# A hybrid decoder block: attention with the orders of three engines written out, and the gates' first products ahead for seven pairs

## The chip, the cores and the metric

The kernel runs on one core of one Trainium2 chip. Its time is device microseconds of one execution; lower is better. A core has a matmul engine (PE, TensorE; its weight loads are listed as PEld), VectorE (DVE), ScalarE (ACT), GpSimd (POOL), SyncE (SP), which only issues DMAs here, and 16 DMA engines. Matmuls read operands from SBUF and write banks of 128 x 512 float32 in PSUM.

## The reference

One layer, 1024 positions, width 1024, all float32:

```python
h = _rmsnorm(x, g_mix_pre[l])
proj = jnp.einsum('bsd,de->bse', h, w_in[l]) + b_in[l]
u_pool, q, k, v, gates = jnp.split(proj, IN_SPLITS, axis=-1)
y_pool = _multiscale_pool(u_pool, w_pool[l], pool_scale[l])
...
y_attn = _sliding_window_sink_attention(
    q.reshape(B, S, N_KV_HEADS, GROUP, HEAD_DIM), k, v, attn_sinks[l])
g = jax.nn.sigmoid(gates.astype(jnp.float32)).astype(x.dtype)
g_pool, g_attn = g[..., :D_MODEL], g[..., D_MODEL:]
merged = (g_pool * jnp.einsum('bsc,cd->bsd', y_pool, w_branch_pool[l])
          + g_attn * jnp.einsum('bsc,cd->bsd', y_attn, w_branch_attn[l]))
mix = jnp.einsum('bsd,de->bse', merged, w_out[l])
x = x + _rmsnorm(mix, g_mix_post[l])
h2 = _rmsnorm(x, g_mlp_pre[l])
ff = jnp.einsum('bsf,fd->bsd',
                jnp.square(jax.nn.relu(jnp.einsum('bsd,df->bsf', h2, w_up[l]))), w_down[l])
x = x + _rmsnorm(ff, g_mlp_post[l])
```

Attention has 8 query heads and 2 key heads of 64, a window of 128 in blocks of 128, and a sink per head in the softmax. The pooling takes, for each of four groups of 128 channels, the mean over the last 2, 4, 8 or 16 positions less the input, and mixes it with a 128 x 128 matrix.

## The kernel before

**Precision.** Every float32 matrix product is done in three passes (hi x hi, hi x lo, lo x hi) of a shorter type, `PASSES`. `split(hi, lo, src)` makes the parts: ScalarE casts (L101), VectorE subtracts (L104), so each operand costs one instruction on either engine, and VectorE's waits for ScalarE's.

**Stages.** The first stage multiplies x by the weights of q, k and v (L179, L188), tiles 0 to 3 while the weights come in. The attention stage (from about 44 us in the profile) takes eight tiles n of 128 positions. `pre_qkv(n)` scales and rotates on VectorE and GpSimd; `post_qkv(n)` transposes q and k and splits them; `score(n, g)` makes scores for one half (g = 0, 1) of the heads, four in number, in a PSUM bank called "sc", of which there is one. ScalarE copies the part of the tile's own keys out of it (L325), and VectorE's copy_predicated (L326) lays the previous tile's keys over it where the mask says so; only then is the bank free for the next half. `softmax(n)` takes maxima on VectorE, eight exponentials on ScalarE (L340), and scales on VectorE (L343). `attend_t(n)` transposes the probabilities (L354), splits them, and multiplies them with a mask (L360); `attend_v(n)` multiplies by v (L369), and ScalarE copies the result to y (L373).

Between these steps `fill(t)` takes matmuls worth t us from a generator, `others()`: q, k and v of tiles 4 to 7, then the products u for the pooling (L538; groups gi = 3, 2, 1, 0, of windows 16, 8, 4, 2), each with a VectorE multiplication (L541) and a ScalarE bias (L542).

`pool_in(gi)` forms the windowed sums of one u on VectorE by doubling (L606, L607), subtracts (L609 to L611) and splits the result; `pool_mix(gi)` multiplies with the mixing matrix (L622 to L624), scales on ScalarE (L625) and spills to DRAM.

**Gates.** The gates' projection (2048 outputs) is done by an algorithm of seven block products for each pair p = 0 to 7 of weight blocks (`class Pairs`). Products 1 and 2 take x itself, the others sums and differences of x that `build_gate(kt)` makes in four steps from freshly loaded x (L678 to L684). `prepare(p)` loads a weight block and splits the operands of products 1 and 2. `m1(p)` is product 1 (12 matmuls, L461); ScalarE copies its bank to f0 (L468, the changed kernel's L487). `m2(p)` adds product 2 on top in the same bank, and VectorE scales the sum into f0. `rest(p)` does the other five products (60 matmuls). For pairs 0 to 4 (`NG0 = 5`) m1 and m2 stand ahead, among pooling and `build_gate`: this stretch, from about 182 to 225 us, is called the gate front here. Pairs 5 to 7 do all seven in the loop of rests, which begins at 225 us. After the gates come the branches, the output product and the MLP, which are the same in both kernels.

**Order.** In the attention stage a `manual_schedule` holds PE to the order in which the code stands; VectorE, ScalarE and the whole gate front are ordered by the framework's scheduler. Each engine then works through its queue in order. The results f0 take slots of a pool "yy" of four, which y and the pooling sums also use. DMAs are issued by SyncE's queue, or by ScalarE's (`nc.scalar.dma_start`).

Of the kernel before, what the change touches and what calls it, by code (L numbers as in the profile page):

```python
# [14 lines left out]
P = 128  # L15
# [35 lines left out]
def block_kernel(ctx: ExitStack, tc, xt, x, consts, vecs, sinks, b_qkv, g_post, g_mlp, g_mlp_post,  # L51
# [227 lines left out]
    def post_qkv(n):  # L279
        tf = tfs.pop(n)  # L280
        t = tf[:, :768].rearrange("p (h d) -> p h d", d=HD)
        bt, bk = bank("at"), bank("at")
# [24 lines left out]
    def score(n, g):  # L307
# [18 lines left out]
        dve.copy_predicated(s4, wide(from_prev), sb[:, :, :, :P] if n else wide(neg))  # L326

    soft = {}

    def softmax(n):  # L330
# [7 lines left out]
        act.activation(es, es, AF.Exp)  # L338
        for h in range(NH):
            act.activation(s8[:, h], s8[:, h], AF.Exp, scale=SCALE, bias=nmx[:, h:h + 1], accum_out=den[:, h:h + 1])  # L340
        dve.tensor_tensor(den, den, es, ALU.add)
# [5 lines left out]
    def attend_t(n):  # L347
# [8 lines left out]
        pc = None  # L356
        if n:
            pc = [at("s4", 4, [NH, P], F32R) for _ in range(2)]
            for t, s in zip(pc, pt):
                dve.tensor_tensor(t, f32(s), own_t.unsqueeze(1).broadcast_to([P, NH, P]), ALU.mult)  # L360
        probs[n] = pt, pc
# [146 lines left out]
    us, wu = {}, {}  # L508
# [3 lines left out]

    def others():
        for qs, kvs in (((4,), (4,)), ((5,), (5,)), ((6, 7), (6, 7))):
            for n in qs:
                bq[n] = bank("mm")
                for k in range(NK):
                    mm_q(n, k, bq[n])
                    yield 3 * 0.227
            if n == NT - 1:  # L520
                wu[3] = load_w(w_u[3], [NK, P])
            for n in kvs:
                bkv[n] = bank("at" if n == 4 else "mm", [1, 256])
                for k in range(NK):
                    mm_kv(n, k)
                    yield 3 * 0.12
                pre_qkv(n)
        for gi in (3, 2, 1, 0):
            if gi:
                wu[gi - 1] = load_w(w_u[gi - 1], [NK, P])  # L530
            whi, wlo = wu.pop(gi)
            u = ga_.tile([P, S], F32, tag="ga", name=nm("u"))
            for th in range(2):
                sl = slice(th * 512, (th + 1) * 512)
                b = bank("mm")
                for k in range(NK):
                    for j, (xh, h) in enumerate(PASSES):
                        pe.matmul(b, (whi, wlo)[h][:, k, :], xr(k, xh, th), start=k == 0 and j == 0,  # L538
                                  stop=k == NK - 1 and j == 2)
                    yield 3 * 0.227  # L540
                dve.tensor_tensor(u[:, sl], b, rb[:, sl], ALU.mult)  # L541
            act.activation(u, u, AF.Identity, bias=vec[:, V_BU + gi:V_BU + gi + 1])  # L542
            us[gi] = u
# [13 lines left out]
    with tc.manual_schedule(engines={mybir.EngineType.PE}):  # L557
        for n in range(4):
            pre_qkv(n)
        fill(8.3)  # L560
        post_qkv(0)
        make_rb()
        score(0, 0)
        fill(2.5)
        post_qkv(1)
        score(0, 1)
        softmax(0)
        fill(3.0)
        score(1, 0)
        fill(2.5)  # L570
        post_qkv(2)
        score(1, 1)
        softmax(1)
        fill(5.5)
        for n in range(NT):
            attend_t(n)
            fill(2.5)
            if n + 2 < NT:
                score(n + 2, 0)
            fill(2.0)  # L580
            if n + 2 < NT:
                score(n + 2, 1)
                softmax(n + 2)
            if n + 3 < NT:
                post_qkv(n + 3)
            fill(2.5)
            attend_v(n)
            if n % 4 == 3:
                for kh in range(2):
                    nc.sync.dma_start(y_dram[n // 4 * 2 + kh], flat(y[n // 4][kh]))  # L590
        fill(1e3)


    wps = stage([4, P])
    nc.sync.dma_start(wps, w_pool)
# [114 lines left out]
    for p in (3, 4):  # L710
        gt.m1(p, bank("mm"), g32([S]))
        gt.m2(p)
# [563 lines left out]
```

## Time and profile before

| | |
|---|---|
| median of 3 runs | 1154.15 us (1153.27 to 1158.45) |
| profiled execution | 1154.03 us, of which the span of instructions is 1152.2 us |
| PE | 1120.7 us busy (97%), 5202 matmuls |
| VectorE, ScalarE | 820.4 us (71%), 525.1 us (46%) |
| GpSimd | 70.0 us (6%) |
| DMA | 179.06 MB, mean 155 GB/s |

A row of a timeline gives start and duration in us, engine, line, operation and tiles, the count, and in brackets the idle time before it with the instruction that ended it. A row of waits gives engine, tile and line that waited, what it waited for, us in total, times, and the longest. In a row of a group of instructions, the total busy time and the mean ns of one follow the bar. Durations overlap a little where instructions of one engine are pipelined; what counts is the distance from one start to the next. PEclk is the clock granted to TensorE, 1.00 at full speed. Lines are those of the kernel before unless said otherwise.

### The profile page before, as it was taken

What the parts mean: (1) busy time and instruction counts of PE and PEld (TensorE: products, weight loads), DVE (VectorE), ACT (ScalarE), POOL (GpSimd) and SP (SyncE); (2) the same over time, 40 slices, a digit from 0 to 9 for tenths busy, and PEclk for the clock granted to TensorE, in tenths of its full rate; (3) what the DMA queues carried; (4) which work ended last, traced back from release to release, by engine and by line L of the source; (5) the groups of instructions that cost most, each with busy time, mean ns of one, the idle gap of its engine ahead of it and who ended that gap; (6) DMA issues with size and microseconds to landing.
All of it is one profiled execution on the core that took longest, in us unless ns stands there. A gap on an engine that the chain in (4) does not pass through costs nothing.

```text
span 1152.2 us, 13954 instructions
## 1 busy us (share of the span) xinstructions
PE 1120.7 (97%) x5202; PEld 925.8 (80%) x5202; DVE 820.4 (71%) x1209; ACT 525.1 (46%) x912; POOL 70.0 (6%) x110
## 2 busy tenths in 40 slices
PE   7999998899999999999999999999999999999997
PEld 6877776788888888888788888888888888888885
DVE  7677797998654585767997766666557945446887
ACT  7354556544332233364655444535344345344342
POOL 3523110000000150000000000000000000000000
PEclk9999999999999999999999999999999999999999
DMA  7210106544345453333256434343788665432652
GB/s 261 74 46 19 56 19 249 189 165 146 123 168 185 149 199 110 139 127 120 92 220 219 170 132 177 125 179 123 266 296 290 222 194 180 130 92 73 205 190 99
DMA packets 66163, 179.06 MB, mean 155 GB/s; under 512 B 6192, under 2 KB 6192, under 8 KB 66096
## 3 DMA queue, kind: packets, MB, share of 16 engines
q1 hardware_dynamic: 60336, 157.73, 39.8%
q10 hardware_dynamic: 5760, 20.45, 4.5%
q8 instruction: 41, 0.67, 0.2%
q14 instruction: 26, 0.21, 0.1%
HBM read 127.82 MB, written 50.33 MB: 155 GB/s over the span
## 4 chain that ended last, share of the span: by engine, by line
PE 85%; DVE 9%; ACT 3%; DMA 2%; issue 1%; SPq 0%; DVEq 0%
PE mm L461 20%; PE at L461 16%; PE at L1114 14%; PE mm L1114 11%; PE mm L831 5%; PE mm L398 5%; PE mm L179 3%; PE mm L400 3%; PE at L188 1%; PE sc L179 1%; DVE s L360 1%; ACT s L340 1%; PE at L831 1%; PE mm L538 1%; PE sc L323 1%
## 5 line engine op out<-in xcount | busy, mean ns | idle before, releaser
L1114 PE MATMUL at<-ar,wh 128*128 128x512 f32 x744 | 169.5, 389 | 0.0
L1114 PEld LDWEIGHTS at<-ar,wh 128*128 128x128 f32 x744 | 139.6, 188 | 29.3 <-DVE ar L104 0.4
L1114 PE MATMUL mm<-ar,wh 128*128 128x512 f32 x576 | 131.0, 389 | 0.0
L1114 PEld LDWEIGHTS mm<-ar,wh 128*128 128x128 f32 x576 | 108.1, 188 | 22.5
L101 ACT CAST wh<-st 128x512 fp32r<-128x512 f32 (+1 forms) x106 | 67.0, 642 | 123.7 <-PE mm L398 34.1
L104 DVE TENSOR_TENSOR wh<-raw,wh 128x1024 fp32r<-128x1024 f32 x53 | 64.8, 1223 | 80.9 <-ACT wh L101 80.5
L101 ACT CAST wh<-raw 128x1024 fp32r<-128x1024 f32 x53 | 55.8, 1053 | 131.1 <-PE at L1114 62.6
L104 DVE TENSOR_TENSOR wh<-st,wh 128x512 fp32r<-128x512 f32 (+1 forms) x106 | 82.9, 788 | 16.4 <-ACT wh L101 14.0
L461 PE MATMUL mm<-gr,wh 128*128 128x512 f32 x300 | 72.1, 390 | 0.0
L461 PE MATMUL mm<-T,wx 128*128 128x512 f32 x288 | 67.6, 389 | 0.0
L461 PEld LDWEIGHTS mm<-gr,wh 128*128 128x128 f32 x300 | 56.1, 188 | 11.6
L461 PEld LDWEIGHTS mm<-T,wx 128*128 128x128 f32 x288 | 54.1, 188 | 11.2
L461 PE MATMUL at<-T,wx 128*128 128x512 f32 x252 | 59.1, 389 | 0.0
L461 PE MATMUL mm<-x,wh 128*128 128x512 f32 x216 | 52.5, 399 | 3.5 <-ACT g L468 3.5
L461 PEld LDWEIGHTS at<-T,wx 128*128 128x128 f32 x252 | 47.3, 188 | 9.8
L461 PEld LDWEIGHTS mm<-x,wh 128*128 128x128 f32 x216 | 41.6, 193 | 12.8 <-ACT g L468 3.9
L104 DVE TENSOR_TENSOR ar<-B,ar 128x1024 fp32r<-128x1024 f32 x37 | 45.0, 1217 | 9.4 <-ACT ar L101 9.4
L538 PE MATMUL mm<-x,wh 128*128 128x512 f32 x192 | 48.7, 404 | 0.0
L461 PE MATMUL at<-gr,wh 128*128 128x512 f32 x183 | 44.2, 389 | 0.0
L101 ACT CAST ar<-B 128x1024 fp32r<-128x1024 f32 x37 | 38.8, 1050 | 11.1 <-DMA B<-in_w_dn_dram 6.2
L538 PEld LDWEIGHTS mm<-x,wh 128*128 128x128 f32 x192 | 35.7, 192 | 7.6
L748 DVE TENSOR_TENSOR g<-g,mm 128x512 f32<-128x512 f32 x32 | 20.5, 683 | 28.3 <-PE mm L400 28.2
(350 smaller groups left out, 2204.3 us busy)
## 6 DMA issues: line engine op xcount, KB each, us to landing
raw<-f_dram SPq DMA_DIRECT2D x53, 512.0 KB, 3.6
f_dram<-g SPq DMA_DIRECT2D x30, 512.0 KB, 3.3
B<-in_w_dn_dram SPq DMA_DIRECT2D x24, 512.0 KB, 5.7
st<-in_w_up_dram SPq DMA_DIRECT2D x22, 512.0 KB, 3.5
f_dram<-g ACTq DMA_DIRECT2D x17, 512.0 KB, 2.6
st<-in_w_g_dram SPq DMA_DIRECT2D x16, 512.0 KB, 3.8
g<-spill_dram SPq DMA_DIRECT2D x16, 512.0 KB, 4.3
raw<-in_w_dn_dram SPq DMA_DIRECT2D x16, 512.0 KB, 4.5
```

The lines of the kernel that those rows point to most:

```text
L101: act.copy(hi, src)
L104: eng.tensor_tensor(lo, src, f32(hi), ALU.subtract)
L179: pe.matmul(bq, xs_[k][n // 4][:, xh, n % 4 * P:(n % 4 + 1) * P], wq[k][:, h, :], start=k == 0 and j == 0, stop=k == NK - 1 and j == 2)
L188: pe.matmul(bkv_of(n), xs_[k][n // 4][:, xh, n % 4 * P:(n % 4 + 1) * P], wkv[k // 2][:, h, k % 2, :], start=k == 0 and j == 0 and not (joi ...
L323: pe.matmul(sb[:, kv, i, :nk], qt[r, qx, m * P:(m + 1) * P], kx[r, k0:k0 + nk], start=j == 0, stop=j == 2)
L398: pe.matmul(bs[th], whi[:, k, :], rhs(k, hl, th), start=k == 0 and hl == 0, stop=False)
L400: pe.matmul(bs[th], wlo[:, k, :], rhs(k, 0, th), start=False, stop=k == nk - 1)
L461: pe.matmul(b, w[:, wh, kt, :], xo[kt][:, xh, :], start=not after and kt == 0 and j == 0, stop=kt == 3 and j == 2, skip_group_check=after)
L538: pe.matmul(b, (whi, wlo)[h][:, k, :], xr(k, xh, th), start=k == 0 and j == 0, stop=k == NK - 1 and j == 2)
L748: dve.tensor_tensor(z[:, sl], z[:, sl], bs[th], ALU.mult)
L831: pe.matmul(obs[n][dj], l, wos[k][whl][:, dj * 512:(dj + 1) * 512], start=k == 0 and hl == 0 and whl == 0, stop=k == NK - 1 and hl == 1)
L1114: pe.matmul(bs[t], fo[fh][:, k2, t * P:(t + 1) * P], wo_[wh][:, k2, :], start=not after and s2 == 0 and k2 == 0 and j == 0, stop=s2 == NS ...
```

## The change

In the attention stage the order is now given for VectorE and ScalarE too. `score` no longer issues its masked copy; it is a step of its own (`score_prev`), as are the parts of softmax (`softmax_max`, `softmax_exp` in two halves of the heads, `softmax_scale`) and the mask multiplication (`attend_own`). `pool_in` is a generator whose steps are placed in the tiles: `pool_in(3)` in tiles 4 to 6, `pool_mix(3)` and three steps of `pool_in(2)` in tile 7. What `others()` leaves for VectorE and ScalarE (splits of weights, biases) is put off to `flush_late()`. The matmuls of u take the high weights for all of x first and then the low ones. The fills have other sizes. `post_qkv(0)` uses the "sc" bank.

In the gate front PE's order is given too: m2 of a pair directly follows its m1, the pool mixes and steps of `build_gate` stand between pairs. `NG0` is 7: pairs 5 and 6 have m1 and m2 ahead as well, their f0 is stored to DRAM through ScalarE's queue and loaded again, one rest ahead, through SyncE's queue.

```diff
@@ -279,7 +279,11 @@
...
-        bt, bk = bank("at"), bank("at")
+        if n:
+            bt, bk = bank("at"), bank("at")
+        else:
+            b = bank("sc", [2, 512])
+            bt, bk = b[:, 0], b[:, 1]
...
@@ -323,11 +327,15 @@
...
-        dve.copy_predicated(s4, wide(from_prev), sb[:, :, :, :P] if n else wide(neg))
-    soft = {}
-    def softmax(n):
+        prev[n, g] = s4, sb[:, :, :, :P] if n else wide(neg)
+    prev, soft = {}, {}
+    def score_prev(n, g):
+        s4, other = prev.pop((n, g))
+        dve.copy_predicated(s4, wide(from_prev), other)
+    def softmax_max(n):
...
@@ -335,9 +343,17 @@
...
-        act.activation(es, es, AF.Exp)
-        for h in range(NH):
+        soft[n] = s8, nmx, es, den
+    def softmax_exp(n, heads):
+        s8, nmx, es, den = soft[n]
+        if heads[0] == 0:
+            act.activation(es, es, AF.Exp)
+        for h in heads:
             act.activation(s8[:, h], s8[:, h], AF.Exp, scale=SCALE, bias=nmx[:, h:h + 1], accum_out=den[:, h:h + 1])
+    def softmax_scale(n):
+        s8, nmx, es, den = soft.pop(n)
...
@@ -353,12 +369,15 @@
...
-        pc = None
+        probs[n] = pt, None
+    def attend_own(n):
         if n:
+            pt = probs[n][0]
...
-        probs[n] = pt, pc
+            probs[n] = pt, pc
...
@@ -505,42 +524,64 @@
...
-    us, wu = {}, {}
+    us, wu, d = {}, {}, {}
+    late = []
+    def flush_late():
+        while late:
+            late.pop(0)()
...
+    def load_u(gi):
+        ws = stage([NK, P])
+        nc.sync.dma_start(ws, w_u[gi])
+        def parts():
+            wu[gi] = wslot([NK, P]), wslot([NK, P])
+            split(*wu[gi], ws)
+        late.append(parts)
     def others():
-        for qs, kvs in (((4,), (4,)), ((5,), (5,)), ((6, 7), (6, 7))):
-            for n in qs:
-                bq[n] = bank("mm")
-                for k in range(NK):
-                    mm_q(n, k, bq[n])
-                    yield 3 * 0.227
+        for n in range(4, NT):
+            flush_late()
+            bq[n] = bank("mm")
+            for k in range(NK):
+                mm_q(n, k, bq[n])
+                yield 3 * 0.227
             if n == NT - 1:
-                wu[3] = load_w(w_u[3], [NK, P])
-            for n in kvs:
-                bkv[n] = bank("at" if n == 4 else "mm", [1, 256])
-                for k in range(NK):
-                    mm_kv(n, k)
-                    yield 3 * 0.12
+                load_u(3)
+                flush_late()
+            bkv[n] = bank("at" if n == 4 else "mm", [1, 256])
+            for k in range(NK):
+                mm_kv(n, k)
+                yield 3 * 0.12
+            if n == 4:
+                late.append(lambda: pre_qkv(4))
+            else:
                 pre_qkv(n)
         for gi in (3, 2, 1, 0):
+            flush_late()
             if gi:
-                wu[gi - 1] = load_w(w_u[gi - 1], [NK, P])
+                load_u(gi - 1)
...
-                for k in range(NK):
-                    for j, (xh, h) in enumerate(PASSES):
-                        pe.matmul(b, (whi, wlo)[h][:, k, :], xr(k, xh, th), start=k == 0 and j == 0,
-                                  stop=k == NK - 1 and j == 2)
-                    yield 3 * 0.227
+                mms = [(k, xh, 0) for k in range(NK) for xh in range(2)] + [(k, 0, 1) for k in range(NK)]
+                for j, (k, xh, h) in enumerate(mms):
+                    pe.matmul(b, (whi, wlo)[h][:, k, :], xr(k, xh, th), start=j == 0, stop=j == len(mms) - 1)
+                    if j % 2:
+                        yield 2 * 0.227
                 dve.tensor_tensor(u[:, sl], b, rb[:, sl], ALU.mult)
-            act.activation(u, u, AF.Identity, bias=vec[:, V_BU + gi:V_BU + gi + 1])
-            us[gi] = u
+            def bias(u=u, gi=gi):
+                act.activation(u, u, AF.Identity, bias=vec[:, V_BU + gi:V_BU + gi + 1])
+                us[gi] = u
+            late.append(bias)
...
@@ -554,50 +595,8 @@
...
-    with tc.manual_schedule(engines={mybir.EngineType.PE}):
-        for n in range(4):
-            pre_qkv(n)
-        fill(8.3)
-        post_qkv(0)
-        make_rb()
-        score(0, 0)
-        fill(2.5)
-        post_qkv(1)
-        score(0, 1)
-        softmax(0)
-        fill(3.0)
-        score(1, 0)
-        fill(2.5)
-        post_qkv(2)
-        score(1, 1)
-        softmax(1)
-        fill(5.5)
-        for n in range(NT):
-            attend_t(n)
-            fill(2.5)
-            if n + 2 < NT:
-                score(n + 2, 0)
-            fill(2.0)
-            if n + 2 < NT:
-                score(n + 2, 1)
-                softmax(n + 2)
-            if n + 3 < NT:
-                post_qkv(n + 3)
-            fill(2.5)
-            attend_v(n)
-            if n % 4 == 3:
-                for kh in range(2):
-                    nc.sync.dma_start(y_dram[n // 4 * 2 + kh], flat(y[n // 4][kh]))
-        fill(1e3)
-    wps = stage([4, P])
-    nc.sync.dma_start(wps, w_pool)
-    wpt = bcp.tile([P, 2, 4, P], F32R, tag="bc", name="wpt")
-    split(wpt[:, 0], wpt[:, 1], wps)
-    d = {}
     def pool_in(gi):
...
@@ -606,12 +605,15 @@
...
+            yield
...
+        yield
...
+        yield
...
@@ -625,12 +627,78 @@
...
-    pool_in(3)
-    pool_mix(3)
-    pool_in(2)
-    pool_mix(2)
-    pool_in(1)
-    pool_in(0)
+    LOW, HIGH = range(4), range(4, 8)
+    with tc.manual_schedule(engines={mybir.EngineType.PE, mybir.EngineType.DVE, mybir.EngineType.Activation}):
+        pre_qkv(0)
+        pre_qkv(1)
+        fill(5.4)
+        post_qkv(0)
+        pre_qkv(2)
+        fill(2.8)
+        score(0, 0)
+        score_prev(0, 0)
+        pre_qkv(3)
+        score(0, 1)
+        score_prev(0, 1)
+        post_qkv(1)
+        softmax_max(0)
+        make_rb()
+        softmax_exp(0, range(3))
+        fill(3.0)
+        score(1, 0)
+        score_prev(1, 0)
+        softmax_exp(0, range(3, 8))
+        post_qkv(2)
+        fill(0.7)
+        score(1, 1)
+        softmax_scale(0)
+        score_prev(1, 1)
+        softmax_max(1)
+        fill(3.7)
+        for n in range(NT):
+            attend_t(n)
+            if n == 0:
+                softmax_exp(1, LOW)
+            if n + 1 < NT:
+                softmax_exp(n + 1, HIGH)
+            if n + 2 < NT:
+                score(n + 2, 0)
+            attend_own(n)
+            if n + 2 < NT:
+                score_prev(n + 2, 0)
+            if n + 1 < NT:
+                softmax_scale(n + 1)
+            flush_late()
+            if n == NT - 1:
+                pool_mix(3)
+            fill(3.6)
+            if n + 2 < NT:
+                score(n + 2, 1)
+                score_prev(n + 2, 1)
+                softmax_max(n + 2)
+            if n + 3 < NT:
+                post_qkv(n + 3)
+            if n + 2 < NT:
+                softmax_exp(n + 2, LOW)
+            if n == 3:
+                wps = stage([4, P])
+                nc.sync.dma_start(wps, w_pool)
+                wpt = bcp.tile([P, 2, 4, P], F32R, tag="bc", name="wpt")
+                late.append(lambda: split(wpt[:, 0], wpt[:, 1], wps))
+            if n == 4:
+                p3 = pool_in(3)
+            if n == NT - 1:
+                p2 = pool_in(2)
+            for _ in range({4: 1, 5: 2, 6: 9}.get(n, 0)):
+                next(p3, None)
+            for _ in range({7: 3}.get(n, 0)):
+                next(p2, None)
+            fill(1e3 if n == NT - 1 else 4.1)
+            attend_v(n)
+            if n % 4 == 3:
+                for kh in range(2):
+                    nc.sync.dma_start(y_dram[n // 4 * 2 + kh], flat(y[n // 4][kh]))
+        flush_late()
...
@@ -690,26 +758,41 @@
...
-    gt.prepare(0)
-    gt.prepare(1)
-    gt.prepare(2)
-    build_gate(0)
-    gt.m1(0, bank("mm"))
-    gt.m1(1, bank("mm"))
-    build_gate(1)
-    pool_mix(1)
-    pool_mix(0)
-    build_gate(2)
-    gt.m2(0)
-    gt.m2(1)
-    gt.prepare(3)
-    gt.m1(2, bank("mm"))
-    gt.m2(2)
-    build_gate(3)
-    gt.prepare(4)
-    for p in (3, 4):
-        gt.m1(p, bank("mm"), g32([S]))
-        gt.m2(p)
+    def finish(steps):
+        for _ in steps:
+            pass
+    finish(p2)
+    for p in range(3):
+        gt.prepare(p)
+    NG0 = 7
+    with tc.manual_schedule(engines={mybir.EngineType.PE}):
+        for p in range(2):
+            gt.m1(p, bank("mm"))
+            gt.m2(p)
+        pool_mix(2)
+        finish(pool_in(1))
+        build_gate(0)
+        gt.m1(2, bank("mm"))
+        gt.m2(2)
+        pool_mix(1)
+        finish(pool_in(0))
+        gt.prepare(3)
+        build_gate(1)
+        gt.prepare(4)
+        gt.m1(3, bank("mm"), g32([S]))
+        gt.m2(3)
+        pool_mix(0)
+        build_gate(2)
+        gt.m1(4, bank("mm"), g32([S]))
+        gt.m2(4)
+        build_gate(3)
+        for p in (5, 6):
+            gt.prepare(p)
+            gt.m1(p, bank("mm"))
+            gt.m2(p)
+            nc.scalar.dma_start(z_dram[2 * p], gt.f0.pop(p))
...
@@ -722,8 +805,10 @@
...
-    NG0 = 5
     for p in range(8):
+        if p + 1 in (5, 6):
+            gt.f0[p + 1] = gate_result()
+            nc.sync.dma_start(gt.f0[p + 1], z_dram[2 * p + 2])
...

```

## Prediction

> **What bounds the kernel now.** I read the page's head and its chain first, then the busy time in stretches chosen at the stage borders, then what the matmul engine (PE) waited for.
>
> ```profile
> span 1152.2 us, 13954 instructions
> ...
> PE 85%; DVE 9%; ACT 3%; DMA 2%; issue 1%; SPq 0%; DVEq 0%
> ```
>
> ```profile
> core 0: us, PE busy (x) PEld busy (x) DVE busy (x) ACT busy (x) POOL busy (x), PEclk, DMA share, GB/s
> 43.85:100.00 56.15, 51.83 (x351) 44.27 (x351) 37.42 (x69) 26.69 (x83) 20.23 (x49) 0.97 0.08 24
> 100.00:160.00 60.00, 56.00 (x328) 44.77 (x327) 50.05 (x82) 30.90 (x104) 16.26 (x32) 1.00 0.12 45
> 160.00:181.60 21.60, 21.60 (x105) 18.06 (x104) 20.26 (x32) 11.80 (x32) 0.00 (x0) 1.00 0.05 17
> 181.60:225.05 43.45, 35.70 (x146) 27.86 (x144) 36.77 (x59) 28.85 (x47) 0.00 (x0) 0.96 0.71 259
> 225.05:1150.00 924.95, 917.85 (x4073) 758.00 (x4071) 643.46 (x935) 399.13 (x603) 17.47 (x12) 1.00 0.48 166
> ```
>
> The work that ended last is PE's for 85% of the span, and behind 225 us PE has next to nothing left to win: it idles there 7.1 of 925 us. What the change reorders lies in 43.85 to 225.05 us. There PE idles 4.32 + 4.00 us in the attention stage (first two rows; the third has no gap) and 7.75 us in the gate front. A granted clock below 1 costs about 0.03 x 51.83 = 1.55 us in the first row and 0.04 x 35.70 = 1.43 us in the fourth. The attention stage thus loses 9.9 us, the gate front 9.2 us, together **19.1 us**: no reordering can win more, as the number of matmuls stays at 5202.
>
> ```profile
> PE sc L323 <- DVE s L326: 7.7, 5, 2.7
> ...
> PE mm L461 <- ACT g L468: 3.5, 1, 3.5
> PE at L623 <- DVE ar L104: 3.2, 2, 2.2
> PE at L622 <- ACT ar L101: 1.1, 1, 1.1
> ```
>
> The waits name the causes. In attention it is score's second half (L323), which needs the bank that VectorE's masked copy (L326) has to free; in the gate front it is the pooled sums (L622, L623) and once ScalarE's copy of a first product (L468). The chain of work from 140 to 160 us, by line, shows what holds the masked copy up:
>
> ```profile
> by line: DVE t L606 23.9%; DVE s L360 11.3%; PE mm L538 11.3%; DVE s L326 6.5%; DVE s L104 5.8%; PE at L369 5.7%; DVE s L343 5.7%; DVE nmx L335 5.6%; DVE u L609 5.5%; DVE wh L104 5.2%; PE sc L323 4.9%; DVE t L607 3.6%; DVE qt L104 2.8%; iss
> ```
>
> The pooling sums (L606, L607, L609) are 33% of it: they stand between softmax's steps in VectorE's order.
>
> **Attention: three orders by hand.** The pooling sums no longer slip in ahead of the masked copies, and 3.6 us of other matmuls stand between a tile's two halves of score. What is left is worked out from these rows.
>
> ```profile
> L326 DVE COPY_PREDICATED s<-cst,sc 128x512 f32<-128x512 uint32 x14 | 10.2, 729 | 4.5 <-ACT s L325 4.5
> ...
> L340 ACT ACTIVATE s<-s,nmx 128x128 f32<-128x128 f32 x64 | 24.8, 389 | 14.4 <-DVE nmx L336 14.4
> ...
> L325 ACT COPY s<-sc 128x512 f32<-128x512 f32 x16 | 9.4, 586 | 27.0 <-PE sc L323 27.0
> ```
>
> ```profile
> 177.44 1.21 DVE L606 TENSOR_TENSOR t<-t 128x1022 f32<-128x1022 f32 x1
> 178.58 0.16 DVE L607 COPY t<-t 128x2 f32<-128x2 f32 x1
> ...
> 213.09 0.74 DVE L682 SCALAR_TENSOR_TENSOR g<-g,vec,g 128x512 f32<-128x512 f32 x1
> 213.76 0.68 DVE L104 TENSOR_TENSOR T<-xr,T 128x512 fp32r<-128x512 f32 x1
> ...
> 216.29 2.49 DVE L104 TENSOR_TENSOR gr<-g,gr 128x512 fp32r<-128x512 f32 x4
> 218.70 1.28 DVE L104 TENSOR_TENSOR T<-xr,T 128x512 fp32r<-128x512 f32 x2
> ```
>
> From start to start a 1024-column VectorE operation takes 178.58 - 177.44 = 1.14 us, a 512-column one (218.70 - 216.29)/4 = 0.60, the fused one 0.67.
> Tile 0: score(0,1) stands right behind score(0,0) and waits for copy and masked copy, 0.59 + 0.73 and hand-overs of about 0.1: 1.4 us. Tile 1: about 0.25. In step n = 0 ScalarE has two casts and eight exponentials (8 x 0.389 = 3.1 us) ahead of the copy of score(2,0); with copy and masked copy that ends some 6.2 us after the tile's transposes begin, and PE has 0.79 + 0.91 + 3.6 = 5.3 us of work: 0.9. In n = 1 to 5 VectorE has 2 x 0.60 + 2 x 1.14 + 0.73 = 4.2 us from the first cast on, about 1.1 us after the transposes begin: 5.3 against PE's 5.3, so 0 to 0.4 a tile, say 1.0 in all. Sum about **3.6 us**, bounds 2 and 5, each too short for the clock to drop as it did behind the stall of 2.40 below. Attention wins 9.9 - 3.6 = **6.3 us**.
>
> **Gate front: m2 right behind m1.** Each of seven pairs now has its second product directly behind the first. The first matmul of m2 writes the bank which ScalarE's copy of m1 still reads, and before the change other matmuls stood in between. Nothing covers the copy now, but for 4 and 10 matmuls of the first rest at pairs 5 and 6.
>
> ```profile
> 95.75 0.39 PE L323 MATMUL sc<-klo,qt 64*128 64x256 f32 x2 [2.40 <-DVE s L326]
> ...
> 97.78 3.97 PE L538 MATMUL mm<-x,wh 128*128 128x512 f32 x12
> 101.59 0.63 PE L369 MATMUL at<-s,v 128*128 128x512 f32 x2
> ...
> 155.68 0.39 PE L323 MATMUL sc<-klo,qt 64*128 64x256 f32 x2 [2.66 <-DVE s L326]
> ...
> 172.57 1.03 PE L354 MATMUL at<-cst,s 128*128 128x128 f32 x8
> 173.36 0.94 PE L538 MATMUL mm<-x,wh 128*128 128x512 f32 x3
> ...
> 186.94 5.60 PE L461 MATMUL mm<-x,wh 128*128 128x512 f32 x24
> 192.38 0.39 PE L622 MATMUL at<-ar,wpt 128*128 128x512 f32 x1
> ...
> 217.85 7.36 PE L461 MATMUL mm<-x,wh 128*128 128x512 f32 x24 [3.47 <-ACT g L468]
> 225.05 1.29 PE L461 MATMUL at<-gr,wh 128*128 128x512 f32 x5
> ```
>
> ```profile
> 215.13 2.18 ACT L101 CAST gr<-g 128x512 fp32r<-128x512 f32 x4 [1.00 <-DVE g L683]
> 217.22 1.06 ACT L468 COPY g<-mm 128x512 f32<-128x512 f32 x2
> ```
>
> A matmul goes by (192.38 - 186.94)/24 = 0.227 us. The least price of a pair is the last matmul's 0.16 us beyond its slot, the copy's 0.53 and hand-overs: 0.85 us. The last two rows show what makes it more: the copies at 217.22 began as soon as ScalarE was through with four casts, and those had waited for VectorE; PE meanwhile stood for 3.47 us. In the new ScalarE order each copy of pairs 2, 3 and 4 stands behind such casts: the copy of m1(4) behind four that take VectorE's last product for operand kt = 2.
>
> So I count what VectorE must do by then. From the start of tile 7's transposes (call it 0) to that product its order holds 33 operations of 512 columns (19.8 us), 12 fused (8.0), 14 of 1024 columns (16.0) and 12 small ones (1.4): 45.2 us, behind about 2.65 us which it still owes attention (pool sum 3). PE's work in the same stretch is 0.79 us of transposes and 176 matmuls (32 of u, 12 of attention's last product, 24 in four pool mixes, 96 of pairs 0 to 3, 12 of m1(4)): 40.7 us. Behind VectorE's last product lie the last cast and the copy, 1.1 us. Whatever the single waits are, their sum up to m2(4) is VectorE's time + 1.1 - 40.7.
>
> ```profile
> 172.57:217.20 44.63, 37.53 (x165) 29.73 (x163) 38.02 (x59) 28.84 (x47) 0.00 (x0) 1.00 0.65 236
> ...
> 200.00:220.00 20.00, 16.53 (x72) 13.36 (x71) 19.30 (x32) 12.65 (x22) 0.00 (x0) 0.98 0.58 211
> ...
> 240.00:260.00 20.00, 20.00 (x90) 16.56 (x89) 17.67 (x29) 9.74 (x14) 0.00 (x0) 1.00 0.54 184
> ```
>
> VectorE's own gaps decide. In the same stretch before it was busy 38.02 of 44.63 us, 0.85; in its densest 20 us there 19.30, 0.965. At 0.85 the sum is 45.2/0.85 + 2.65 + 1.1 - 40.7 = 16.2 us, at 0.965 it is 9.9, without any gap 8.3, at 0.80 it is 19.6. I take 0.87, near the row of the same stretch, a little up as some of that row's gaps were waits for pool mixes that come later now: **15.0 us**. Going along the queues pair by pair gives nearly that: pool mix 1.7, m2(0) 3.3, m2(1) 0.8, m2(2) 1.2, m2(3) 3.4, m2(4) 5.5. Behind m2(4): m2(6) waits for a buffer that a spill to DRAM must leave, and the first rest for one more spill: 0 to 3, I take 1.0. The stall of 5.5 should halve the clock as 3.47 did, whose 24 matmuls took 7.20 us and not 5.44: 1.76, I take 1.5. Gate front 15.0 + 1.0 + 1.5 = 17.5 us against 9.2: **8.3 us lost**.
>
> **The clock.** Of the stalls before, 2.40 was followed by slow matmuls (12 in 3.81 us and not 2.72: 1.1 lost) and 3.47 too; 2.66 was not (PEclk 1.00 in its stretch). [...]
>
> **The rest loop.** Pairs 5 and 6 leave 24 matmuls each out of it and bring two reloads.
>
> ```profile
> g<-spill_dram SPq DMA_DIRECT2D x16, 512.0 KB, 4.3
> ...
> g<-in_xt_dram SPq DMA_DIRECT2D x6, 512.0 KB, 6.0
> ```
>
> A rest without its first two products is 60 x 0.227 = 13.6 us; the reload is issued a rest ahead and needs 4.3 (second row, for later: 6.0 for the loads of x). With 60 matmuls a rest, VectorE was busy 17.67 of 20 us at 240 to 260 while PE had no gap. So both rests cost nothing beyond PE's work, which only moves. If that cover goes (reload behind other loads on SyncE's queue, 2 x 6.0), it costs 2 us at most each.
>
> **Sum.** 1154.03 us (the profiled execution's own time; median of three runs 1154.15) - 6.3 + 8.3 = **1156.0 us**.
>
> **Rivals.**
> - *VectorE closes up.* Its queue has a backlog at all times, as the 19.30 of 20 show it can. Front 9.9 + 1.0 = 10.9 with no stall long enough for the clock, attention 3.0: 13.9 against 19.1, -5.2; with no gap at all and attention at 2: 8.3 + 0.5 + 2 = 10.8, -8.3, 1146; the floor of the argument, with attention at 0, is -10.8. For it: the pool sums are spread evenly now. Against: 0.85 over 44.63 us, where VectorE waited for ScalarE and the loads by turns. It wins where density is above 0.95. Time about **1147**.
> - *The clock falls behind every long wait.* m2(0), m2(3) and m2(4) stand over 3 us and each is followed by at least 24 matmuls at half rate: 3 x 1.76 = 5.3 where I took 1.5; that begins at waits of 2.4 to 3.5 us. Loads of x at 6.0 lengthen those waits, together some 4 us more by my walk along the queues. 1156 + 3.8 + 4 = **1164**. For it: 3.47 and 2.40 paid. Against: 2.66 did not.
> - *Attention stays as it was.* VectorE's 50.05 of 60 us at 100 to 160 is its real limit and the masked copy is late wherever it stands: 6.3 us are not won: **1162**. Against: a third of the chain there was pooling sums, which now stand behind the masked copies.
>
> **How the numbers follow.** About 0.5% (5.8 us) is what a measurement of this kernel can tell from no change. Likeliest case 0.45 (1150 to 1162: density 0.82 to 0.93; of it 0.03 faster, 0.36 same, 0.06 slower); VectorE closes up 0.27 (0.24 faster, 0.03 same); clock 0.16 (all slower); attention as before 0.12 (0.05 same, 0.07 slower). Faster 0.27, same 0.44, slower 0.29. The range from 1144 (close to the floor) to 1166 leaves some 2 in 10 out.
>
> **What would show it.** Right: after the change the waits list has ScalarE's copy of the first product (now L487) on top with 8 us or more and several events, score's waits sum to about 3.6 us, and tile 7's transposes begin near 164 us. Each step wrong: score's waits above 6; L487's below 6 us; a reload of pairs 5 and 6 in the list of waits. The time is wrong above all if VectorE's share between tile 7's transposes and the first rest is above 0.95 or below 0.80.

## The result, and the profile after

The changed kernel takes 1159.86 us (median of 20 runs, 1157.87 to 1162.93) against 1155.47 us (20 runs, 1153.27 to 1160.58): ratio 1.0031, interval 1.0020 to 1.0042. It is slower, by less than the 0.5% named. The profiled execution took 1161.2 us, 7.2 us more than that of before.

Busy time of the changed kernel in stretches at its own stage borders: attention up to tile 7's transposes (164.57 us), tile 7, the gate front, the rest.

```profile
43.85:100.00 56.15, 53.88 (x363) 44.98 (x363) 37.41 (x73) 28.61 (x99) 22.12 (x56) 0.97 0.02 7
100.00:164.57 64.57, 64.57 (x366) 52.71 (x365) 53.34 (x85) 34.27 (x112) 8.66 (x25) 1.00 0.15 52
164.57:181.60 17.03, 13.20 (x55) 10.35 (x54) 13.37 (x21) 6.32 (x10) 0.00 (x0) 0.90 0.27 93
181.60:240.70 59.10, 48.23 (x184) 37.65 (x183) 44.80 (x72) 31.56 (x50) 0.00 (x0) 0.88 0.56 202
240.70:1157.00 916.30, 909.06 (x4033) 750.57 (x4031) 639.71 (x928) 397.94 (x599) 17.47 (x12) 1.00 0.48 169
```

What PE waited for, the changed kernel:

```profile
PE mm L480 <- ACT g L487: 7.7, 2, 4.6
PE sc L179 <- ACT wh L101: 6.2, 1, 6.2
PE at L624 <- ACT y L392: 3.7, 1, 3.7
PE mm L480 <- ACT z L487: 3.1, 3, 1.7
PE at L480 <- DVE f_first L512: 1.1, 1, 1.1
PE sc L327 <- DVE den L357: 0.8, 1, 0.8
```

In attention PE now idles 2.27 us (56.15 - 53.88; no gap behind 100 us) where it was 8.32. From tile 7 to 240.7 us it idles 3.83 + 10.87 us, and the slow clock costs 0.10 x 13.20 + 0.12 x 48.23 = 7.1 us more, where before had 7.75 and 1.43. Behind the gates nothing has changed: from the first matmul of the branch stage to the end it is 801.9 us here and 802.0 before. That stage's start, 350.2 us before and 357.5 after, is used below as the mark of where front and rests end.

Of the 7.2 us between the two profiled executions, 1.6 (0.03 x 53.88) are a slow clock between 41 and 50 us, where PE waited 0.17 us. Another execution with the same code there ran at full clock (last section), so nothing shows them to be the change's doing.

PE's own timeline shows the three longest waits and what the clock makes of each:

```profile
164.57 1.03 PE L370 MATMUL at<-cst,s 128*128 128x128 f32 x8
169.29 0.50 PE L624 MATMUL at<-ar,wpt 128*128 128x512 f32 x1 [3.68 <-ACT y L392]
...
171.96 8.14 PE L576 MATMUL mm<-x,wh 128*128 128x512 f32 x32
...
211.81 5.49 PE L480 MATMUL mm<-x,wh 128*128 128x512 f32 x12 [3.17 <-ACT g L487]
217.09 0.63 PE L624 MATMUL at<-ar,wpt 128*128 128x512 f32 x1
...
226.26 8.17 PE L480 MATMUL mm<-x,wh 128*128 128x512 f32 x24 [4.57 <-ACT g L487]
234.26 1.07 PE L480 MATMUL at<-gr,wh 128*128 128x512 f32 x4
```

m2(3)'s 12 matmuls take 217.09 - 211.81 = 5.28 us and not 2.72; the 24 from 226.26 take 8.00 and not 5.44. Each of the two waits is followed by 2.56 us of slow clock; the granted clock is 0.50 from 211.81 to 217.09 us and from 226.26 to 230.

Two queue orders stand behind these waits: ScalarE's behind the first, SyncE's in the chain of work that leads to the other two. ScalarE's timeline, and SyncE's queue:

```profile
164.62 1.05 ACT L101 CAST ar<-u 128x1024 fp32r<-128x1024 f32 x1 [5.00 <-DVE u L611]
167.56 1.15 ACT L582 ACTIVATE u<-u,vec 128x1024 f32<-128x1024 f32 x1 [1.90 <-DVE u L579]
168.62 0.62 ACT L392 COPY y<-at 128x256 f32<-128x256 f32 x2
```

```profile
160.92 21.67 SPq L444 DMA_DIRECT2D st<-in_w_g_dram  x4
183.72 0.80 SPq L700 DMA_DIRECT2D spill_dram<-y  x2
184.61 1.92 SPq L744 DMA_DIRECT2D g<-in_xt_dram  x2
```

The copies of attend_v(6)'s result, whose bank pool_mix(3) wants, were ready to run at 164.7 but stand behind a bias of u that waits for VectorE until 167.56. And the first loads of x for build_gate are issued at 184.61, behind four loads of weights and the stores of y. The last of the four waits 16.1 us for VectorE and goes at 182.26; the stores wait another 1.1 us for the copies of attend_v(7)'s result. The chain of work between 164 and 226 us has that load in it: 6.4 us.

```profile
184.61 6.37 DMA g<-in_xt_dram
191.06 1.16 ACT g L746
```

### The profile page after: what moved, and what is told of

It reads as the page before. It is cut to its first block, busy times and chain, and to the rows that moved or that the text cites. A ratio compares the mean times of both kernels' runs of the same rounds, so it can differ in the third digit from the quotient of the medians.

```text
span 1159.4 us, 13966 instructions
## 1 busy us (share of the span) xinstructions
PE 1126.5 (97%) x5202; PEld 928.9 (80%) x5202; DVE 821.2 (71%) x1209; ACT 526.6 (45%) x912; POOL 64.3 (6%) x110
## 4 chain that ended last, share of the span: by engine, by line
PE 82%; DVE 8%; ACT 4%; DMA 2%; issue 2%; SPq 0%; DVEq 0%; ACTq 0%
PE mm L480 19%; PE at L480 15%; PE at L1199 14%; PE mm L1199 11%; PE mm L916 5%; PE mm L417 5%; PE mm L576 3%; PE mm L419 3%; PE mm L179 2%; PE at L388 1%; DVE wh L104 1%; PE sc L327 1%; PE at L916 1%; DMA st<-in_w_up_dram 1%; DVE T L104 1%
## 5 line engine op out<-in xcount | busy, mean ns | idle before, releaser
L480 PE MATMUL mm<-x,wh 128*128 128x512 f32 x240 | 62.9, 416 | 10.9 <-ACT g L487 7.7
L480 PEld LDWEIGHTS mm<-x,wh 128*128 128x128 f32 x240 | 48.0, 202 | 23.5 <-ACT g L487 8.6
L576 PE MATMUL mm<-x,wh 128*128 128x512 f32 x192 | 47.1, 400 | 0.0
L576 PEld LDWEIGHTS mm<-x,wh 128*128 128x128 f32 x192 | 36.0, 191 | 8.1
```

Of the source, the lines that this page charges most:

```text
L480: pe.matmul(b, w[:, wh, kt, :], xo[kt][:, xh, :], start=not after and kt == 0 and j == 0, stop=kt == 3 and j == 2, skip_group_check=after)
L576: pe.matmul(b, (whi, wlo)[h][:, k, :], xr(k, xh, th), start=j == 0, stop=j == len(mms) - 1)
```

## The experiments

Two theories were put against each other. **Local** (theory 1): each wait has its own cause in a queue's order, and goes when that order goes. **VectorE's total** (theory 2): VectorE's work sets when the front ends, as the prediction summed it, so that a wait removed in one place returns further on. "Before" is the kernel before in the same runs; m2(4) is the start of its first matmul, counted from tile 7's transposes; the branch stage's start is that of the profiled execution. Both columns come from one execution each. The runs were made in four groups, each with its own runs of before, so kernels are compared by their ratios.

| kernel | median us (before) | ratio, interval | m2(4) | branch stage |
|---|---|---|---|---|
| before | 1155.47 | | | 350.2 |
| the change | 1159.86 (1155.47) | 1.0031, 1.0020 to 1.0042 | 61.7 | 357.5 |
| e1_attention_only | 1156.34 (1155.14) | 1.0006, 0.9990 to 1.0021 | | 349.6 |
| e2_copies_first | 1158.09 (1155.14) | 1.0022, 1.0006 to 1.0037 | 57.4 | 353.9 |
| e3_five_pairs | 1156.96 (1155.14) | 1.0006, 0.9992 to 1.0021 | | 351.2 |
| e4_mix_later | 1149.99 (1155.14) | 0.9944, 0.9923 to 0.9966 | 51.4 | 347.0 |
| e5_busy_pe | 1159.20 (1154.50) | 1.0043, 1.0031 to 1.0055 | 60.1 | 355.6 |
| e6_copies_covered | 1157.56 (1154.50) | 1.0024, 1.0010 to 1.0037 | 58.5 | 353.5 |
| e7_bias_behind_y | 1156.47 (1154.50) | 1.0010, 0.9997 to 1.0022 | 56.4 | 351.5 |
| e8_later_five_pairs | 1153.41 (1154.50) | 0.9994, 0.9982 to 1.0005 | 53.0 | 347.7 |
| e9_later_old_front | 1150.11 (1154.18) | 0.9959, 0.9941 to 0.9976 | | 345.3 |
| e10_two_firsts | 1156.34 (1154.18) | 1.0012, 0.9997 to 1.0027 | 56.6 | 354.2 |
| e11_other_slot | 1155.69 (1154.18) | 1.0003, 0.9987 to 1.0019 | 56.4 | 351.0 |
| e12_x_ahead | 1152.64 (1153.73) | 0.9987, 0.9971 to 1.0002 | 47.8 | 343.5 |

**The attention stage alone (e1).** The front is the listing of before.

> The changed attention stage with the gate front of before (pairs 0 to 4 ahead, order of the front left to the scheduler, no DRAM detour). Theory 1 (each wait is local: what a stage loses is its own): the attention stage keeps its gain of 6.0 us, so about 1149.5 us against 1155.5. Theory 2 (VectorE's queue sets when the front ends, so that what attention wins comes back as waits of the front, since VectorE enters tile 7 with some 4 us more work owed): 1152 to 1154 us, with 3 to 4 us more of PE waits behind tile 7's transposes than before's 7.75.

Measured 1156.3, no gain at all. Tile 7's transposes begin at 162.88 us, 9.7 us earlier than before with 1.8 us less of u done, so attention did win; PE's timeline shows where it went:

```profile
167.60 0.79 PE L624 MATMUL at<-ar,wpt 128*128 128x512 f32 x1 [3.68 <-ACT y L392]
...
183.43 0.73 PE L624 MATMUL at<-ar,wpt 128*128 128x512 f32 x2 [2.72 <-ACT ar L101]
...
216.17 8.49 PE L480 MATMUL mm<-x,wh 128*128 128x512 f32 x24 [3.72 <-ACT g L487]
```

The wait ahead of pool_mix(3), a part of the changed attention, and the slow clock behind it (0.91 from 160 to 200 us) take most of it. Both expectations missed, theory 2 by less.

**The copies ahead of the casts (e2).**

```diff
-        build_gate(0)
         gt.m1(2, bank("mm"))
+        build_gate(0)
         gt.m2(2)
...
-        build_gate(1)
-        gt.prepare(4)
         gt.m1(3, bank("mm"), g32([S]))
+        build_gate(1)
+        gt.prepare(4)
         gt.m2(3)
         pool_mix(0)
-        build_gate(2)
         gt.m1(4, bank("mm"), g32([S]))
+        build_gate(2)
```

> The changed kernel, PE's order untouched, but each build_gate step is issued behind the next m1, so that on ScalarE the copies of m1(2), m1(3), m1(4) stand ahead of the casts they stood behind. Theory 1 (the copies behind VectorE-fed casts are the price): the waits for m1(3)'s and m1(4)'s copies fall from 3.17 and 4.57 us to 1 to 1.5 each and the slow clock behind both goes (2.6 us each): 6 to 10 us less, 1150 to 1154. Theory 2 (VectorE's chain sets the end of the front): the waits move to the first rest or to the next pair, and the time falls by less than 3 us: 1157 to 1160.

m2(3)'s wait fell from 3.17 to 0.70 us, as theory 1 says, but m1(4)'s copy now stood behind the casts of the build before, and m2(4)'s wait rose to 5.71. Behind tile 7's transposes VectorE was busy 43.22 us up to m2(4) and idle 14.15, so it was not VectorE's work that took the gain back: on SyncE's queue the loads of x for kt = 1 were issued at 208.59 us, in the change at 191.02. The ratio is 0.0009 below the change's, about 1 us and inside the intervals: theory 2's figure, by another queue order.

**Five pairs (e3) and the pool mix behind u (e4).**

```diff
-    NG0 = 7
+    NG0 = 5
...
-        for p in (5, 6):
-            gt.prepare(p)
-            gt.m1(p, bank("mm"))
-            gt.m2(p)
-            nc.scalar.dma_start(z_dram[2 * p], gt.f0.pop(p))
...
-        if p + 1 in (5, 6):
-            gt.f0[p + 1] = gate_result()
-            nc.sync.dma_start(gt.f0[p + 1], z_dram[2 * p + 2])
```

> The changed kernel with pairs 5 and 6 back in the loop of rests, so without the two stores and reloads through DRAM. Theory 1 (the two pairs cost and bring nothing): 1159 to 1161. Theory 2 (their 48 matmuls cover the time until VectorE has the first rest's operands): the first rest waits 1 to 4 us more, 1161 to 1164. Rival (the detour itself costs, through queues and slots): 1155 to 1158.

> The changed kernel with pool_mix(3) behind the 3.6 us of u matmuls of tile 7 in place of ahead of them. Its wait of 3.68 us is then covered and the slow clock behind it (about 1.3 us) goes. Theory 1 (local waits): about 5 us less, 1155. Theory 2 (VectorE sets the end of the front): the 5 us come back at m2(0) to m2(4), 1158 to 1160, with the start of m2(4) within 1.5 us of where it was, 61.7 us behind tile 7's transposes.

```diff
-            if n == NT - 1:
-                pool_mix(3)
             fill(3.6)
+            if n == NT - 1:
+                pool_mix(3)
```

e3: 0.0025 of the ratio better than the change, some 3 us, within the rival's range: in this order the two pairs ahead cost, their products and the detour through DRAM taken together. e4: 10 us better than the change and 0.56% better than before. Its timeline of PE:

```profile
169.06 0.50 PE L624 MATMUL at<-ar,wpt 128*128 128x512 f32 x1 [0.25 <-DVE s L104]
...
181.93 7.39 PE L480 MATMUL mm<-x,wh 128*128 128x512 f32 x24 [2.83 <-ACT z L487]
...
205.88 3.02 PE L480 MATMUL mm<-x,wh 128*128 128x512 f32 x12 [0.85 <-ACT g L487]
...
214.55 5.74 PE L480 MATMUL mm<-x,wh 128*128 128x512 f32 x24 [1.57 <-ACT g L487]
```

The wait ahead of pool_mix(3) is gone, and m2(3) and m2(4) wait 0.85 and 1.57 us where they waited 3.17 and 4.57. m2(4) begins 10.3 us earlier. But more was changed than the edit shows. The scheduler answered it with other orders for VectorE and ScalarE (the last build, kt = 3, now stands behind m1(4)'s copy) and for SyncE, whose queue issues the first load of x ahead of the stores of y, 20 us earlier than in the change:

```profile
164.79 0.38 SPq L744 DMA_DIRECT2D g<-in_xt_dram  x1
176.82 0.80 SPq L700 DMA_DIRECT2D spill_dram<-y  x2
```

So VectorE does not have the same work ahead of m2(4). From tile 7's transposes to m2(4), in the change and in e4 (the third busy time is VectorE's):

```profile
164.57:226.26 61.69, 46.99 (x186) 36.44 (x184) 49.56 (x78) 34.91 (x55) 0.00 (x0) 0.90 0.55 195
163.13:214.55 51.42, 44.37 (x185) 34.42 (x183) 45.26 (x72) 31.73 (x51) 0.00 (x0) 0.97 0.60 210
```

Of the 10.3 us, 4.3 are work of VectorE that now comes later, and 6.0 are idle time of VectorE that is gone (12.13 against 6.16).

**PE kept busy (e5).** The first products of pairs 3 and 4 are done twice.

```diff
+            if again:
+                self.mm(b, p, 1, range(again))
             self.mm(b, p, 1)
...
-        gt.m1(3, bank("mm"), g32([S]))
+        gt.m1(3, bank("mm"), g32([S]), again=4)
...
-        gt.m1(4, bank("mm"), g32([S]))
+        gt.m1(4, bank("mm"), g32([S]), again=4)
```

> The changed kernel with the 12 matmuls of m1(3) and of m1(4) done twice (24 matmuls of 2.72 us each pair more than needed, into the same bank): PE works where it stood waiting for 3.17 and 4.57 us. If the slow clock comes from the wait, it goes at m2(3) and shortens at m2(4): the waits fall to about 0.5 and 1.9 us, the 24 matmuls behind take 2.72 us a dozen and not 5.3, and the time falls by about 5 us to 1154 to 1156, although PE does 5.4 us more. If the clock does not hang on the wait, or VectorE sets the end of the front, the time stays within 1.5 us of 1159.9 or rises.

```profile
212.06 3.02 PE L480 MATMUL mm<-x,wh 128*128 128x512 f32 x12 [0.68 <-ACT g L489]
...
224.77 7.35 PE L480 MATMUL mm<-x,wh 128*128 128x512 f32 x24 [2.89 <-ACT g L489]
231.96 1.07 PE L480 MATMUL at<-gr,wh 128*128 128x512 f32 x4
```

PE does 5.4 us more, and m2(4) begins 1.6 us earlier. The slow clock behind m2(3) is gone, that behind m2(4) is 7.19 - 5.44 = 1.75 us and not 2.56. That fits a clock that hangs on PE's waiting, but one execution does not show it: in e3 and e7 the same 12 matmuls ran at full clock behind waits of 3.13 and 3.17 us. The time itself is that of the change: the ratio is 0.0012 above its, inside the intervals, and the branch stage begins 1.9 us earlier in the profile. The 5 us expected did not come: m1(4)'s copy still stood behind the same casts of ScalarE, so that the clock gained ahead of them mostly went into m2(4)'s wait.

**Copies covered by the pool mixes (e6), and only the first two pairs (e10).** Both with pool_mix(3) behind u. In e6 all of this, in e10 the first hunk alone:

```diff
-        for p in range(2):
-            gt.m1(p, bank("mm"))
-            gt.m2(p)
+        gt.m1(0, bank("mm"))
+        gt.m1(1, bank("mm"))
+        gt.m2(0)
+        gt.m2(1)
...
-        gt.m2(2)
         pool_mix(1)
+        gt.m2(2)
...
-        gt.m2(3)
         pool_mix(0)
+        gt.m2(3)
```

> The kernel with pool_mix(3) behind u (1150.0), and in PE's order other matmuls between m1 and m2: m1(0), m1(1), m2(0), m2(1); pool_mix(1) between m1(2) and m2(2); pool_mix(0) between m1(3) and m2(3). Theory of local waits: the waits of 2.83 (m2(0), with the slow clock behind it 1.7), 0.68, 0.82 and 0.85 us go nearly wholly, 5 to 6 us, 1144 to 1146. Theory of VectorE's queue: its products stay where they are and the waits come back at m2(4) or the first rest, 1148 to 1150.

> The kernel with pool_mix(3) behind u (1150.0) and of the reordering only its first part: m1(0), m1(1), m2(0), m2(1), the pool mixes left where they were. If the gain there (48 matmuls without a gap where waits of 2.83 and 0.68 us and 1.7 us of slow clock lay) was eaten up by the pool mixes moved ahead of their sums, it stays now: 1145 to 1147. If VectorE's queue takes it back at m2(3) and m2(4) all the same: 1149 to 1151.

Both lost 8 to 9 us against e4 by the ratios, more than either theory gave. In e6 the covering products were themselves not ready (first two rows, the pooling sums). In e10 pairs 0 and 1 run without a gap, yet m2(3) and m2(4) wait 5.32 us each (last two rows).

```profile
202.48 0.50 PE L624 MATMUL at<-ar,wpt 128*128 128x512 f32 x1 [1.72 <-ACT ar L101]
...
205.00 0.80 PE L625 MATMUL at<-ar,wpt 128*128 128x512 f32 x1 [2.02 <-DVE ar L104]
```

```profile
208.81 4.36 PE L480 MATMUL mm<-x,wh 128*128 128x512 f32 x12 [5.32 <-ACT g L487]
222.56 8.62 PE L480 MATMUL mm<-x,wh 128*128 128x512 f32 x24 [5.32 <-ACT g L487]
```

SyncE's queue in e10 has three loads of weights, which wait for staging buffers, ahead of the loads of x for kt = 1; those are issued at 196.86 us, 30.9 behind tile 7's transposes, in e4 at 25.6. That alone did not put m2(4) off: m2(3) begins 42.8 us behind tile 7's transposes in both. From m2(3) to m2(4) it is then 13.8 us in e10 and 8.7 in e4; in e10 most of the last build stands ahead of m1(4)'s copy again, and VectorE is busy 49.73 us up to m2(4), where e4 has 45.26.

```profile
181.41 15.39 SPq L444 DMA_DIRECT2D st<-in_w_g_dram  x3
196.86 0.90 SPq L744 DMA_DIRECT2D g<-in_xt_dram  x2
```

**The bias behind the copies of y (e7).** pool_mix(3) stays where the change put it; the order of ScalarE's other work in the front is that of the change.

```diff
-            late.append(bias)
+            biases.append(bias)
...
             flush_late()
+            while biases:
+                biases.pop(0)()
             if n == NT - 1:
                 pool_mix(3)
```

> The changed kernel with pool_mix(3) where it was, but the biases of u issued one step later, so that in tile 7 ScalarE copies attend_v(6)'s result (which frees pool_mix(3)'s bank) before it turns to the bias that waits for VectorE. Then the wait of 3.68 us ahead of pool_mix(3) falls to about 0.9 and a wait of 0.4 for VectorE's low part follows. If that one queue order is the cause of the long wait, the time falls by 2.4 us and the slow clock's 1.3, to 1155 to 1156, or further if VectorE's later work moves up with it as with pool_mix(3) behind u (10 us). If not, 1159 to 1160.

```profile
166.50 0.49 PE L624 MATMUL at<-ar,wpt 128*128 128x512 f32 x1 [0.65 <-ACT y L392]
...
208.33 3.01 PE L480 MATMUL mm<-x,wh 128*128 128x512 f32 x12 [3.17 <-ACT g L487]
...
221.25 7.09 PE L480 MATMUL mm<-x,wh 128*128 128x512 f32 x24 [5.82 <-ACT g L487]
```

The wait of 3.68 falls to 0.65, so that one queue order was its cause. The ratio falls by 0.0021, some 2.4 us, where about 4 were expected: m2(4)'s wait takes back 1.25 us. VectorE's work up to m2(4) is that of the change, yet m2(4) begins 5.3 us earlier, as VectorE idles 7.06 us and not 12.13:

```profile
164.82:221.25 56.43, 42.97 (x186) 33.36 (x184) 49.37 (x78) 34.91 (x55) 0.00 (x0) 1.00 0.58 211
```

This is the plainest sign that VectorE's total does not set the end of the front. Of e4's 10 us 7 to 8 are left over; they go with the scheduler's other orders, which were not tried one by one.

**Five pairs with the mix behind u (e8), the old front (e9), another buffer (e11).** e8 joins the edits of e3 and e4, e9 those of e1 and e4; e11 is e10 with this:

```diff
-            gt.m1(p, bank("mm"))
+            gt.m1(p, bank("mm"), g32([S]) if p == 6 else None)
```

> pool_mix(3) behind u and pairs 5 and 6 back in the loop of rests. If the detour through DRAM costs by its slots, m2(6)'s wait of 2.16 us and the slow clock behind it (about 1) go: 1146 to 1148. If the 48 matmuls cover VectorE's work ahead of the first rest, the first rest waits more: 1151 to 1153.

> The changed attention stage with pool_mix(3) behind u, and the gate front of before. If the wait ahead of pool_mix(3) is what took the attention's gain back (1156.3 with it in place), it comes out now: 3.7 us of wait and 1.3 to 1.5 of slow clock less, 1150 to 1152; the new front then brings nothing beside it. If the old front loses it further on, 1154 to 1156, and the new front is worth the 4 to 6 us between this and 1150.0.

> As the two firsts, and pair 6's result in another pool's buffer, so that its copy need not wait for the store of an earlier result to DRAM. m2(6)'s wait of 2.16 us and about 1 us of slow clock behind it go: 2 to 3 us less than the two firsts. If that pool's buffers are wanted elsewhere (loads of weights for the rests wait for them), the same time or up to 3 us more.

e8 lies 0.0050 of the ratio above e4, some 6 us and above both figures expected: here pairs 5 and 6 ahead help, where in the change they cost. e9 is as fast as e4: with the attention's one bad wait gone, the new front brings nothing measurable beside the old. e11 is 0.0009 of the ratio below e10, inside the intervals: in e10's order m2(6) has no wait to lose, and m2(3) and m2(4) wait 4.31 and 5.94 us still. e4 and e9 are the two versions that are clearly faster than both kernels.

**The loads of x one step ahead (e12).** e10 with the loads of build_gate in a function of their own, called before prepare(0) for kt = 0 and 1 and before prepare(3) for kt = 2.

```diff
+    load_x(0)
+    load_x(1)
     for p in range(3):
         gt.prepare(p)
...
+        load_x(2)
         gt.prepare(3)
```

> The kernel of the two firsts (1156.3) with the loads of x for build_gate issued one step earlier, so that on SyncE's queue they stand ahead of the weight loads that wait for staging buffers; by that the casts of the last build (kt = 3) also come behind the copy of m1(4) on ScalarE. If these queue orders are what held the copies of m1(3) and m1(4) for 5.3 us each, the waits fall to 1 to 2 us each and most of the slow clock goes: 1145 to 1149. If VectorE's sum of work sets the end of the front whatever the queues' order, the time stays at 1154 to 1157.

```profile
204.92 3.01 PE L480 MATMUL mm<-x,wh 128*128 128x512 f32 x12 [2.57 <-ACT g L487]
212.70 5.78 PE L480 MATMUL mm<-x,wh 128*128 128x512 f32 x24 [0.69 <-ACT g L487]
```

m2(3)'s and m2(4)'s waits fall from 5.32 each to 2.57 and 0.69, no slow clock follows (1.00 from 200 to 220 us), m2(4) begins 47.8 us behind tile 7's transposes, and the branch stage at 343.5, the earliest of all. As was meant, the last build also stands behind m1(4)'s copy again:

```profile
164.85:212.70 47.85, 42.44 (x186) 33.34 (x184) 44.25 (x71) 30.52 (x50) 0.00 (x0) 1.00 0.60 213
```

Against e10 VectorE has 5.5 us less work ahead of m2(4) and 3.2 us less idle time (3.60 against 6.84). So m2(4) goes with the queues' orders, in two ways: they decide how much of VectorE's work stands ahead of the copy that it needs, and how long VectorE stands idle. Over all the runs with seven or five pairs in the new front, but for e3, VectorE was busy 49.4 to 49.7 us up to m2(4) where the last build stood ahead (the change, e5, e6, e7, e10, e11) and 43.2 to 45.3 where it stood behind (e2, e4, e8, e12); idle it was 3.6 us (e12) to 14.2 (e2). Neither theory holds as it was put: the sum is no constant, and a wait removed in one place did come back in another (e2, e6, e10).

The time is not the 1145 to 1149 expected: a new wait stands far behind, in the MLP, where loads that the scheduler ordered anew come late:

```profile
PE at L1211 <- ACT wh L101: 3.0, 1, 3.0
```

From the branch stage's start to the end it is 807.0 us here, 801.8 to 802.5 in all the others; the wait of 3.0 and the slow clock behind it, where 120 matmuls take 29.15 us and not 27.2, are most of that. Why that order changed was not tried.

## Why the prediction was right or wrong

- **Attention, -6.3.** Right in kind. Idle 2.27 us and 0.03 x 53.88 = 1.6 us of clock are 3.9 us, 3.6 were forecast; tile 7's transposes begin at 164.57, "near 164". That it comes so close is luck: the forecast had waits alone, which came out 1.3 us shorter, and the clock's 1.6 us follow none of them.
- **m2 right behind m1.** Right in kind: waits of 14.71 us up to m2(4). That this is near the 15.0 forecast is luck again, as the bullet after the next shows. Singly, forecast first: pool mix 1.7 / 3.83, m2(0) 3.3 / 0.68, m2(1) 0.8 / 0.79, m2(2) 1.2 / 1.67, m2(3) 3.4 / 3.17, m2(4) 5.5 / 4.57. The pool mix was mis-sized by the bias that stands ahead of the copies of y; m2(0) did not pay, as ScalarE was free when m1(0) ended (it idled 0.59 us ahead of that copy). Behind m2(4) 1.0 was forecast, 0.4 came.
- **The clock, 1.5.** This is the term that was mis-sized: 7.1 us in the front. It was counted for one wait; three paid (3.68, 3.17, 4.57), and 2.56 us each for the last two, not 1.76. It is the loss that the second rival counted, which gave 1164 (with 4 us of longer waits that did not come). No run shows a length of wait from which the clock falls: 2.83 us were followed by 1.65 of loss in e4, 3.17 by none in e7.
- **"VectorE's time + 1.1 - 40.7".** This step held less than its result. PE's 40.7 us are its work at full clock; m2(4) began at 61.7, so waits and slow clock were 21.0 us. VectorE was busy 49.56 of 61.69 us there, 0.80 and not 0.87; at 0.80 the prediction's own sum gives 19.6. The 15.0 was meant for waits and slow clock up to m2(4) together, so it fell short by 6 us. Two errors met: VectorE was slower than taken, and the slow clock took the difference. Nor is that share a cause, or the work a constant: with other orders of ScalarE's and SyncE's queues it was 0.88 (e4, 45.26 of 51.42 us) and 0.92 (e12, 44.25 of 47.85).
- **The rest loop at nothing.** Right for the rests themselves. Pairs 5 and 6 ahead are not free in the front: they cost some 3 us in the change (e3) and bring some 6 in e4's order (e8).
- **Sum.** -6.0 in attention, 14.7 + 0.4 + 7.1 = 22.2 against 9.2 in the front, so 13.0 lost where 8.3 were forecast: +7.0 between the profiled executions, 7.2 measured, 2.0 forecast. Between the medians it is 4.4; 1.6 of the difference can be the clock between 41 and 50 us, the rest is open. The time, 1159.86, lies between the 1156 forecast and the second rival's 1164.

## What to carry to other kernels

A sum of an engine's work tells how late a product may come; in these runs the wait itself hung on what stood ahead of it in another queue's order (PE's 3.68 us behind ScalarE's bias and copies became 0.65 with the two swapped, e7), so look for the one instruction (a bias, a cast, a store) that waits for another engine in front of a short copy which PE needs. Moving one step of PE by 3.6 us of its own work, with the queue orders that the scheduler then chose, gained 10 us, and the whole order written out in the front nothing that could be measured beside it (e9). Where a scheduler orders what the hand does not, an edit's gain is known only with the orders that it then chose: compare the queues of both kernels before naming a cause.

## What the runs showed of the hardware

The slow clock does not follow from a wait's length alone. A wait of 3.17 us was followed by 2.56 us of loss in the change, and the same 3.17 us by none in e7 (the row at 208.33; the next product begins at 211.19, 2.86 us later, where 2.72 is 12 matmuls at full clock); e4 lost 1.65 us behind a wait of 2.83 (24 matmuls in 7.39 us, 5.74 in its row at 214.55). Why equal waits had unlike losses no run here shows.

Runs of one kernel also differ by the clock: the change's run at the highest mean granted clock, 0.995, took 1158.36 us, the one at the lowest, 0.988, 1162.93. One place of it is the stretch from 41 to 50 us, of which PE idled 0.17 us in the change (ahead of 16 matmuls of one column at 41.81) and 0.24 in e4: the changed kernel's profile has 0.81 there, e4's 1.00, with the same code up to that point.

```profile
41.00:50.00 9.00, 8.83 (x43) 7.38 (x42) 4.95 (x15) 2.48 (x4) 2.62 (x7) 0.81 0.01 3
```

```profile
41.00:50.00 9.00, 8.76 (x53) 7.54 (x53) 5.08 (x15) 2.61 (x4) 2.50 (x7) 1.00 0.01 4
```
